# Three parts of a down projection as seven products of quarters, begun three steps late, in a two-layer hybrid trunk on one core

## The chip, the cores and the metric

The kernel runs on one core of one Trainium2 chip. The metric is the device time of one execution in microseconds (us). A profiled execution has, beside its time, a span (first to last instruction), busy times of the engines and the granted clock of the matmul engine. The engines are TensorE (PE; its weight loads are shown as PEld), VectorE (DVE), ScalarE (ACT), GpSimd (POOL) and SyncE (SP). SP and POOL issue the DMAs, and POOL's DMAs can add to what stands in SBUF. Each engine works through its own queue in order.

## The reference, cut to what matters

The trunk has two layers, each a mixer followed by a gated FFN with a short convolution. There are 576 columns (512 of a prompt and 8 sequences of 8), a model width of 1024 and an FFN width of 2816.

```python
for layer in (0, 1):
    x = x + mixer[layer](rmsnorm(x))         # 0: conv module and window attention; 1: Mamba-2
    h = rmsnorm(x)
    g = causal_depthwise_conv3(h @ w_gate)   # 1024 -> 2816
    x = x + (silu(g) * (h @ w_up)) @ w_down  # 2816 -> 1024
```

The change is in how the last product, `@ w_down`, is computed.

## The kernel before, in words

**Layout.** Features lie on partitions, the 576 columns on the free axis. The residual `x` is 8 tiles of 128x576 in float32 (`x[0]` to `x[7]`; in the rows of the order they are `x0_77` to `x7_84`). The FFN width is 22 tiles, numbered f. `HALF` cuts the columns in two halves of 288. A product in float32 is three matmuls on rounded parts (fp32r): high x high, high x low, low x high, where the low half is the original minus the high one. A split is thus one ScalarE copy (the high half) and one VectorE subtraction (the low half).

**Order of the work.** The Python code runs through the instructions in some order, and a tile scheduler with priorities orders each engine's queue. `keep_in_program_order` holds the first matmul of a product in its place.

**Gate and up** (`ffn`, L546). The first tiles (f 0 to 3 of gate, 0 and 1 of up) are done directly at the start. The others go in pairs of f, one job each (`Gate`, `Up`), by the class `Strassen`: quarters of the weights (two f tiles, the two halves of the 1024 rows) times quarters of `h` (halves of rows, halves of columns) in seven products `p1` to `p7` of 12 matmuls (L113, L116, L117), instead of eight. 84 matmuls make a job. The sums of weights are made by DMA: SP loads a quarter into a slot (L68), POOL's accumulating DMA adds the other (L69). `split` (L82, L83) makes the high and low halves, `wl` and `dl` being the low ones. The products accumulate in PSUM banks that are held, `x` and `y`, and in `z`; `keep` (L120) copies intermediate values into SBUF, and the job's `c11`, `c12`, `c22`, `c21` combine them. A pair of jobs (gate of f, f+1 and up of f-2, f-1) yields two more f tiles of silu(gate) x up, the tiles `gsilu`.

**Down.** The 22 f tiles fall into six `PARTS`: f 0 to 1, 2 to 5, 6 to 9, 10 to 13, 14 to 17, 18 to 21. When a part's last tile is there, the loop over the jobs starts its generator `down(p)` (L699): 8 output tiles, each with its own weights (`weights_load` L273, a ring of three buffers `wr`; `single` L293 and L294, two buffers `vh` and `vl`), each in two halves of columns with 4 x 3 matmuls (`mm3` L313, L316, L317), and `add_x` (L497), which adds a PSUM bank to the residual. The generator yields after each half. The loop calls it through `some(1)` four times in a job, so a part takes four jobs, the next part's jobs, while its matmuls stand between the products of gate and up. `up_done` (L581) splits each finished `gsilu` into the pair `yh`, `yl` (L335, L336). The last part goes through `out_proj`, behind the loop.

**SBUF.** `S` hands out slots of 128x576 float32, first in, first out: 48, and 14 more (`EXTRA`) from the first FFN on, 62 in all. Small tiles (`Z`) and the constants of the second mixer (`cst`, 876 columns, loaded through SP at L227, whose second load comes at 172.8 us, before the first FFN begins) are in a pool of their own. The history of the short convolution (`fhist`, `chist`) and the tails that are given back (`fso`, `cso`) have a slot each.

Of the kernel before, what the change touches and what calls it, by code (L numbers as in the profile page):

```python
# [8 lines left out]
F32 = mybir.dt.float32  # L9
F32R = mybir.dt.float32r  # L10
AF = mybir.ActivationFunctionType
# [3 lines left out]
P = 128  # L15
NP = 512
T = 576
HB = 288
DM = 1024
NF = 22  # L20
# [3 lines left out]
LEAD_G, LEAD_U = 4, 2  # L24
PARTS = ((0, 2), (2, 6), (6, 10), (10, 14), (14, 18), (18, 22))


# [13 lines left out]
CV, _n = {}, 0  # L41
# [7 lines left out]
NCV = _n  # L49
# [108 lines left out]
class Builder:  # L158
    NSLOT = 48
    EXTRA = 14  # L160

    def __init__(self, nc, tc, d, stack):
        self.nc, self.tc, self.d = nc, tc, d
        self.const = stack.enter_context(tc.tile_pool(name="const", bufs=1))
        self.xp = stack.enter_context(tc.tile_pool(name="xp", bufs=1))
        self.wp = stack.enter_context(tc.tile_pool(name="wp", bufs=1))
        self.sp = stack.enter_context(tc.tile_pool(name="sp", bufs=1))
        self.pp = stack.enter_context(tc.tile_pool(name="pp", bufs=1, space=bass.MemoryType.PSUM))
        self.dp = stack.enter_context(tc.tile_pool(name="dp", bufs=1, space=bass.MemoryType.DRAM))
        self.rings = {"mm": [0, 1, 2, 3], "aux": [4, 5, 6, 7]}  # L170
        self.idle = list(range(self.NSLOT))
        self.used = {}
        self.held = {}


    def S(self, name, n=T, dt=F32, rows=P):

        i = self.idle.pop(0)
# [11 lines left out]

    def Z(self, name, n, rows=P, bufs=2):
        return self.zp.tile([rows, n], F32, tag=name, bufs=bufs, name=name)

# [23 lines left out]
    def cv(self, name, i=0, n=None, rows=P):  # L217
        o = CV[name] + i
        return self.cst[0:rows, o - self.cst0:o - self.cst0 + n]

    def phase(self, pool, first, last):

        self.zp, self.cst0 = pool, CV[first]
        self.cst = pool.tile([P, (CV[last] if last else NCV) - CV[first]], F32, name="cst")

    def constants(self):
        self.nc.sync.dma_start(self.cst, self.d["cst"][:, self.cst0:self.cst0 + self.cst.shape[-1]])  # L227

# [317 lines left out]
    def ffn(self, l, next_norm):  # L546
        nc, d = self.nc, self.d
        self.rings = {"mm": [0, 1, 2, 3, 4, 5], "aux": [6, 7]}
        hist, so = self.S("fhist", NF * 16), self.S("fso", NF * 16)
        nc.sync.dma_start(hist, d["ffn_hist"][l])  # L550
# [12 lines left out]
        def gate_done(f):  # L563
# [15 lines left out]
            self.free(g, cv)  # L579

        def up_done(f):  # L581
            y_of[f] = self.pair("y")
            self.split(sl_of[f], y_of[f])
            self.free(sl_of.pop(f))

# [113 lines left out]
        def down(p):  # L699
            a, b = PARTS[p]  # L700
            ys = [y_of[f] for f in range(a, b)]
# [10 lines left out]
            def go():  # L712
                nonlocal w
                for m in range(8):
                    now = w
                    if m < 7:
                        w = ready(m + 1)
                    for half in (0, 1):
                        t = self.pm()
                        self.mm3(t[:, :HB], now, range(b - a), ys, HALF[half], pin=True)  # L720
                        self.add_x(m, half, t)
                        if m == 7 and half == 1:
                            self.free([y_of.pop(f) for f in range(a, b)])
                        yield
            return go()

# [13 lines left out]
        for n, job in enumerate(todo + [None]):  # L740
# [42 lines left out]
        nc.sync.dma_start(d["ffn_p"][l], po)  # L783
        self.free(so, hist, self.sr, list(self.hq.values()))
        if next_norm:
            self.norm_begin(*next_norm)
        a, b = PARTS[-1]
        self.out_proj([[d["w_down"][l, m + i][:, a * P:b * P] for i in (0, 1)] for m in range(0, 8, 2)], [y_of[f] for f in range(a, b)],
# [4 lines left out]
    def mix0(self):  # L793
# [181 lines left out]
        self.rings = {"mm": [0, 1, 2, 3], "aux": [4, 5, 6, 7]}  # L975
        self.constants()
        l2 = self.zp.tile([P, P], F32R, tag="l2r", bufs=1, name="l2r")
# [289 lines left out]
    def mix1(self):  # L1267
        nc, d = self.nc, self.d
        hist, so = self.S("chist"), self.S("cso")
        nc.sync.dma_start(hist, d["cc_hist"])  # L1270
# [470 lines left out]
        nc.sync.dma_start(d["cc_p"], po)  # L1741
        self.free(so, hist)
        self.norm_end()
# [7 lines left out]
def build(nc, tc, d):  # L1751
    from contextlib import ExitStack
    with ExitStack() as stack:
        b = Builder(nc, tc, d, stack)
        b.setup()
        with tc.tile_pool(name="segp", bufs=1) as b.segp:
            b.phase(b.segp, "h32", "tri")
# [3 lines left out]
        b.phase(b.ep, "tri", None)  # L1761
        b.ffn(0, ("norm_o", False))
        b.constants()
        b.mix1()
# [159 lines left out]
```

## Time and profile before

| what | value |
|---|---|
| time, median of 3 runs | 1482.84 us (1482.15 to 1484.68) |
| profiled execution: time / span | 1483.3 / 1481.5 us |
| mean granted clock of PE | 0.995 |
| busy: PE, DVE, ACT, POOL | 1459.2, 1119.0, 822.0, 304.1 us |
| matmuls in the trace | 11179 |
| HBM read / written | 190.54 / 15.21 MB |
| matmuls of the down products (`vh`, L313) | 576, from 266.4 to 1452.0 us |

The page gives an engine's busy time, the span in 40 slices, the DMA queues, the chain that ended last and the costliest groups of instructions. In a group, `L313 PE MATMUL mm<-yh,vh` is the line of the kernel, engine, operation, and what it writes from what it reads (buffer numbers left out). Then come the count, busy time, mean duration in ns, and the idle time of the engine just before these instructions, with what ended it. In a timeline, the first two columns are start and duration in us. A row of the table by stage has, for each engine, busy time and number of instructions, then the granted clock of PE (1.00 is full), the DMA share and GB/s.

### The profile page before, as it was taken

Reading aid. Unit: us, or ns where it says so; the run is one execution under the profiler, and the core shown is the slowest. Engines: PE = TensorE matmul, PEld = TensorE weight load, DVE = VectorE, ACT = ScalarE, POOL = GpSimd, SP = SyncE. Lnnn points to the kernel's source line nnn. Section 1 sums busy time; section 2 is a strip of 40 time slices with the busy share of each in tenths; the row PEclk is TensorE's granted clock in tenths of the full one; section 3 lists DMA queues with packets and bytes.
Section 4 is the critical chain, followed back from the end, with each engine's and each line's share of the span. In section 5 each row is a group of like instructions: output and inputs, shape, how many; then the busy total and the mean of one; then the engine's idle time right before and its main releaser. Section 6 shows DMA issues by size and latency. Waiting matters only on the chain.

```text
span 1481.5 us, 29273 instructions
## 1 busy us (share of the span) xinstructions
PE 1459.2 (99%) x11179; PEld 1389.9 (94%) x11179; DVE 1119.0 (76%) x2121; ACT 822.0 (55%) x1659; POOL 304.1 (21%) x517
## 2 busy tenths in 40 slices
PE   8999999999999999999999999999999999999999
PEld 7967799999999999998988998997999999999998
DVE  7968799876666665878897777776989766666673
ACT  6357467655445543487764665665457554444450
POOL 0026211222222220011203102102022222232300
PEclk9999999999999999999999999999999999999999
DMA  7604553787777772136245245245366787877841
GB/s 228 164 29 118 160 133 100 195 212 197 184 200 197 191 191 69 58 121 199 72 154 178 86 124 165 86 146 166 105 172 176 193 217 184 211 195 179 212 113 65
DMA packets 120779, 227.60 MB, mean 154 GB/s; under 512 B 25518, under 2 KB 32558, under 8 KB 120638
## 3 DMA queue, kind: packets, MB, share of 16 engines
q1 hardware_dynamic: 98750, 185.87, 39.7%
q0 software_dynamic: 21888, 39.86, 16.3%
q8 instruction: 88, 1.44, 0.4%
q14 instruction: 53, 0.43, 0.1%
HBM read 190.54 MB, written 15.21 MB: 139 GB/s over the span
## 4 chain that ended last, share of the span: by engine, by line
PE 86%; DVE 6%; ACT 4%; DMA 2%; issue 1%; SPq 0%; ACTq 0%; POOL 0%; DVEq 0%
PE mm L313 15%; PE mm L317 15%; PE mm L316 15%; PE x L113 5%; PE x L116 5%; PE x L117 5%; PE y L116 3%; PE y L117 3%; PE y L113 3%; PE mm L622 2%; PE mm L618 2%; PE mm L621 2%; PE z L116 1%; PE z L113 1%; PE z L117 1%; DMA acb<-acd 1%
## 5 line engine op out<-in xcount | busy, mean ns | idle before, releaser
L313 PE MATMUL mm<-hh,wh 128*128 128x288 f32 x864 | 261.0, 303 | 6.0 <-ACT wh L284 5.4
L316 PE MATMUL mm<-hl,wh 128*128 128x288 f32 x864 | 258.8, 300 | 0.9 <-DVE hl L801 0.8
L317 PE MATMUL mm<-hh,wl 128*128 128x288 f32 x864 | 257.5, 298 | 0.5 <-DVE wl L285 0.5
L497 DVE TENSOR_TENSOR x<-x,mm 128x288 f32<-128x288 f32 x288 | 128.6, 449 | 77.6 <-PE mm L317 76.3
L313 PEld LDWEIGHTS mm<-hh,wh 128*128 128x128 f32 x864 | 163.6, 190 | 14.3 <-ACT wh L284 5.9
L313 PE MATMUL mm<-yh,vh 128*128 128x288 f32 x576 | 170.0, 295 | 0.0
L316 PE MATMUL mm<-yl,vh 128*128 128x288 f32 x576 | 169.9, 295 | 0.0
L317 PE MATMUL mm<-yh,vl 128*128 128x288 f32 x576 | 169.8, 295 | 0.0
L316 PEld LDWEIGHTS mm<-hl,wh 128*128 128x128 f32 x864 | 163.5, 189 | 4.4 <-issue 1.6
L317 PEld LDWEIGHTS mm<-hh,wl 128*128 128x128 f32 x864 | 163.6, 189 | 3.5 <-issue 1.6
L284 ACT ACTIVATE wh<-wr 128x1024 fp32r<-128x1024 f32 (+1 forms) x97 | 101.6, 1048 | 102.6 <-PE mm L316 79.0
L285 DVE TENSOR_TENSOR wl<-wr,wh 128x1024 fp32r<-128x1024 f32 (+1 forms) x97 | 119.5, 1236 | 36.3 <-ACT wh L284 35.5
L82 ACT ACTIVATE wh<-st 128x512 fp32r<-128x512 f32 x152 | 91.3, 626 | 57.8 <-PE z L116 36.0
L69 POOL DMA_DIRECT2D st<-st x76 | 67.5, 889 | 262.8 <-DMA st<-st 65.5
L313 PE MATMUL mm<-yh,wh 128*128 128x288 f32 x384 | 115.9, 302 | 0.7 <-DVE x L497 0.7
L317 PE MATMUL mm<-yh,wl 128*128 128x288 f32 x384 | 115.0, 300 | 0.0
L316 PE MATMUL mm<-yl,wh 128*128 128x288 f32 x384 | 114.9, 300 | 0.0
L83 DVE TENSOR_TENSOR wl<-st,wh 128x512 fp32r<-128x512 f32 x152 | 101.3, 688 | 15.9 <-ACT wh L82 12.3
L316 PEld LDWEIGHTS mm<-yl,vh 128*128 128x128 f32 x576 | 108.4, 188 | 0.0
L317 PEld LDWEIGHTS mm<-yh,vl 128*128 128x128 f32 x576 | 108.3, 188 | 0.0
L313 PEld LDWEIGHTS mm<-yh,vh 128*128 128x128 f32 x576 | 108.3, 188 | 0.0
L573 DVE SCALAR_TENSOR_TENSOR gconv<-gbuf,par,gconv 128x592 f32<-128x592 f32 x88 | 73.0, 832 | 32.2 <-ACT gconv L571 31.6
(409 smaller groups left out, 4306.4 us busy)
## 6 DMA issues: line engine op xcount, KB each, us to landing
st<-in_w_up SPq DMA_DIRECT2D x80, 256.0 KB, 4.3
wr<-in_w_down SPq DMA_DIRECT2D x80, 256.0 KB, 3.5
wr<-in_w_in_o SPq DMA_DIRECT2D x40, 512.0 KB, 3.6
st<-st POOLq DMA_DIRECT2D x76, 256.0 KB, 4.7
st<-in_w_gate SPq DMA_DIRECT2D x72, 256.0 KB, 4.6
wr<-in_w_gate SPq DMA_DIRECT2D x26, 512.0 KB, 4.3
wr<-in_w_up SPq DMA_DIRECT2D x24, 512.0 KB, 4.1
st<-in_w_up POOLq DMA_DIRECT2D x40, 256.0 KB, 4.7
```

The source lines that it names most:

```text
L82: nc.scalar.activation(hi, src, AF.Copy)
L83: nc.vector.tensor_tensor(lo, src, hi.bitcast(F32), op=SUB)
L113: m = nc.tensor.matmul(out, hi[:, ws], xh, start=first and k == 0, stop=False, skip_group_check=skip)
L116: nc.tensor.matmul(out, hi[:, ws], xl, start=False, stop=False, skip_group_check=skip)
L117: nc.tensor.matmul(out, lo[:, ws], xh, start=False, stop=k == 3, skip_group_check=skip)
L284: nc.scalar.activation(hi[:, a:b], raw[:, a:b], AF.Copy)
L285: nc.vector.tensor_tensor(lo[:, a:b], raw[:, a:b], hi[:, a:b].bitcast(F32), op=SUB)
L313: first = nc.tensor.matmul(out, hi[:, ws], xh[:, sl], start=i == 0, stop=False)
L316: nc.tensor.matmul(out, hi[:, ws], xl[:, sl], start=False, stop=False)
L317: nc.tensor.matmul(out, lo[:, ws], xh[:, sl], start=False, stop=i == n - 1)
L497: nc.vector.tensor_tensor(self.x[m][:, sl], self.x[m][:, sl], p[:, :HB], op=ADD)
L573: nc.vector.scalar_tensor_tensor(cv[:, :592], g[:, k:592 + k], w(k), cv[:, :592], op0=MUL, op1=ADD)
```

## The change

Parts 1, 2 and 3 (f 2 to 5, 6 to 9, 10 to 13), in both layers, go through a new generator `down7` in place of `down`.

*Products.* Two output tiles m, m+1 and the part's two halves of f (two tiles each) make four quarters of weights: A11 and A12 are tile m from the first and the second half of f, A21 and A22 tile m+1. The operand's quarters B11, B21 (first and second half of f, first 288 columns), B12, B22 (second 288 columns) are the part's `gsilu`. Seven products of two blocks, 6 matmuls each (`product`, L773, L776, L777 in the changed kernel), do for a pair of output tiles: with A11 on B11 (bank `dx`) and A12 on B21 (bank `mm`); with the first sums of weights on T1 (bank `dy`) and on T2 (`dx`); with the second sums on B22 (`dy`) and on T3 (`dx`); and with A22 on T4 (`dx`). `dx` and `dy` accumulate over several of them, and `add` (L818) adds or subtracts the bank's state behind a product: seven additions of 288 columns for a pair of output tiles, where there were four.

*Operands.* `operand` (L597, L599, L601) writes a high and a low half of 288 columns into one slot (`yq`, or `yT` for the sums T1 to T4, which `combine`, L795, makes in place from the `gsilu` tiles). `up_done` does only the first half of a part's f tiles for such a part; the rest is done by the generator. While a seven-product part runs, the operands of the next part's first half wait until it is over (`waiting`).

*Weights.* `sums` makes two tiles of sums (`sd`) with four additions of 256 columns, and the high and low half of A22 (`dd`, L836). `single` (L306, L307) splits A11 with A12, and each `sd`.

*Three steps late.* The generator yields three times before its first product, while sums and operands are formed.

*SBUF.* `EXTRA` is 19, 67 slots in all, and the added slots of even number hold at most 576 columns, which `S` heeds. `hist` and `so` are one tile in the FFN and in the second mixer. That mixer's small tiles are cut from slots (`small`), its constants stand in two slots (520 and 356 columns) and are loaded when it begins, on SP's queue behind four of the eight last loads of w_down.

```diff
-    EXTRA = 14
+    EXTRA = 19
...
-        hist, so = self.S("fhist", NF * 16), self.S("fso", NF * 16)
+        hist = so = self.S("fhist", NF * 16)
...
+        def operand(name, src, sign=1.0):
+            q = self.S(name, T, F32R)
+            hi, lo = q[:, 0:HB], q[:, HB:T]
+            nc.scalar.activation(hi, src, AF.Copy, scale=sign)
...
+                nc.vector.tensor_tensor(lo, src, hi.bitcast(F32), op=SUB)
...
+        def down7(p):
+            a, b = waiting(p)
+            c = (a + b) // 2
...
+            def sums(m):
+                a11, a12, a21, a22 = [raw[m][:, i * n:i * n + n] for i in range(4)]
+                s12, s43 = s[m, 2], s[m, 3] = self.S("sd", 2 * n), self.S("sd", 2 * n)
+                nc.vector.tensor_tensor(s12[:, 0:n], a21, a22, op=ADD)
+                nc.vector.tensor_tensor(s12[:, n:2 * n], s12[:, 0:n], a11, op=ADD)
+                nc.vector.tensor_tensor(s43[:, n:2 * n], a11, a21, op=ADD)
+                nc.vector.tensor_tensor(s43[:, 0:n], a12, s12[:, n:2 * n], op=ADD)
...
+            def fourth(m):
+                d = last.pop(m)
+                product(x[m][:, :HB], (d[:, 0:n], d[:, n:2 * n]), 0, t["T4"], False)
+                add(m + 1, 0, x[m], SUB)
...
+                sums(0)
+                yield
+                quarters_of("B22")
+                quarters_of("T2")
+                yield
+                split(0, 2)
+                yield
+                for m in range(0, 8, 2):
+                    if m:
+                        fourth(m - 2)
+                    x[m], z = self.ps("dx"), self.pm()
+                    product(x[m][:, :HB], w[m, 1], 0, t["B11"], True)
+                    add(m, 0, x[m], ADD)
+                    product(z[:, :HB], w[m, 1], n, t["B21"], True)
+                    add(m, 0, z, ADD)
+                    split(m, 3)
...
+                    yield
+                    y = self.hold("dy")
+                    product(y[:, :HB], w[m, 2], 0, t["T1"], True)
+                    add(m + 1, 1, y, SUB)
+                    product(x[m][:, :HB], w[m, 2], n, t["T2"], False)
+                    add(m, 1, x[m], ADD)
...
+                    yield
+                    product(y[:, :HB], w[m, 3], 0, t["B22"], False)
+                    add(m, 1, y, ADD)
+                    self.give(y)
+                    product(x[m][:, :HB], w[m, 3], n, t["T3"], False)
+                    add(m + 1, 1, x[m], SUB)
+                    if m < 6:
+                        sums(m + 2)
+                        split(m + 2, 2)
+                    yield
+                fourth(6)
...
-                tiles = down(ready)
+                tiles = (down7 if ready in SEVEN else down)(ready)
...
-        hist, so = self.S("chist"), self.S("cso")
+        self.constants(lambda n: self.S("cst", n), "tri", "selm", None)
+        self.small = []
+        hist = so = self.S("chist")
```

In the built program PE has 10405 matmuls and other entries where it had 10549, DVE 2445 instructions in place of 2121, ACT 1691 in place of 1583, POOL 517 as before, and SP 636 in place of 635.

PE before, the second half of the first output tile of part 1 in layer 0 (`yh`, `yl` are the operand's halves for the four f tiles, `vh`, `vl` the weights'):

```order
L313 MATMUL mm_4153<-yh_3569,vh_4064 128x288
L316 MATMUL mm_4153<-yl_3570,vh_4064 128x288
L317 MATMUL mm_4153<-yh_3569,vl_4065 128x288
L313 MATMUL mm_4153<-yh_3668,vh_4064 128x288
L316 MATMUL mm_4153<-yl_3669,vh_4064 128x288
L317 MATMUL mm_4153<-yh_3668,vl_4065 128x288
L313 MATMUL mm_4153<-yh_3952,vh_4064 128x288
L316 MATMUL mm_4153<-yl_3953,vh_4064 128x288
L317 MATMUL mm_4153<-yh_3952,vl_4065 128x288
L313 MATMUL mm_4153<-yh_4044,vh_4064 128x288
L316 MATMUL mm_4153<-yl_4045,vh_4064 128x288
L317 MATMUL mm_4153<-yh_4044,vl_4065 128x288
```

PE after, the third step of the first pair of output tiles of the same part: the product with B22 (`yq_4149`, `yq_4152`) into `dy` and the one with T3 (`yT_4241`, `yT_4244`) into `dx`:

```order
L773 MATMUL dy_4326<-yq_4149,vh_4237 128x288
L776 MATMUL dy_4326<-yq_4149,vh_4237 128x288
L777 MATMUL dy_4326<-yq_4149,vl_4238 128x288
L773 MATMUL dy_4326<-yq_4152,vh_4237 128x288
L776 MATMUL dy_4326<-yq_4152,vh_4237 128x288
L777 MATMUL dy_4326<-yq_4152,vl_4238 128x288
L773 MATMUL dx_4221<-yT_4241,vh_4237 128x288
L776 MATMUL dx_4221<-yT_4241,vh_4237 128x288
L777 MATMUL dx_4221<-yT_4241,vl_4238 128x288
L773 MATMUL dx_4221<-yT_4244,vh_4237 128x288
L776 MATMUL dx_4221<-yT_4244,vh_4237 128x288
L777 MATMUL dx_4221<-yT_4244,vl_4238 128x288
```

Twelve matmuls on four f tiles that ended in one bank are now two products of six that go on in two banks begun earlier. Behind these rows come the 12 matmuls of `p7` of an up job, and then the product with `dd_4120` (A22 on T4), again into `dx_4221`.

DVE before, from the addition behind these matmuls (the second of that part) to the fourth (`gbuf` and `gconv` belong to a gate job, `st` and `gsilu` also to an up job, `vl` and `wl` are low halves of weights):

```order
L497 TENSOR_TENSOR x0_77<-x0_77,mm_4153 128x288
L573 SCALAR_TENSOR_TENSOR gconv_4146<-gbuf_3999,par_72,gconv_4146 128x592
L641 SCALAR_TENSOR_TENSOR gbuf_4179<-st_3160,x_3912 128x224
L642 SCALAR_TENSOR_TENSOR gbuf_4179<-st_3160,x_3912 128x8x8
L294 TENSOR_TENSOR vl_4188<-wr_4184,vh_4187 128x512
L83 TENSOR_TENSOR wl_4306<-wr_4289,wh_4305 128x1024
L497 TENSOR_TENSOR x1_78<-x1_78,mm_4191 128x288
L659 TENSOR_TENSOR st_3159<-st_3159,z_4205 128x288
L83 TENSOR_TENSOR wl_4310<-st3_4073,wh_4309 128x512
L661 TENSOR_TENSOR gsilu_3761<-gsilu_3761,st_3159 128x288
L83 TENSOR_TENSOR wl_4310<-st2_4072,wh_4309 128x512
L497 TENSOR_TENSOR x1_78<-x1_78,mm_4240 128x288
```

DVE after, from the addition that reads `dy_4326` behind the product with B22 to the split of the next `sd`:

```order
L818 TENSOR_TENSOR x0_77<-x0_77,dy_4326 128x288
L818 TENSOR_TENSOR x1_78<-x1_78,dx_4221 128x288
L307 TENSOR_TENSOR vl_4394<-sd_4381,vh_4393 128x512
L699 SCALAR_TENSOR_TENSOR st_3158<-st_3158,x_4100 128x288
L84 TENSOR_TENSOR dl_4547<-wr_4534,dh_4546 128x512
L703 TENSOR_TENSOR gsilu_3862<-gsilu_3862,st_3158 128x288
L818 TENSOR_TENSOR x1_78<-x1_78,dx_4221 128x288
L818 TENSOR_TENSOR x2_79<-x2_79,dx_4418 128x288
L84 TENSOR_TENSOR wl_4537<-wr_4520,wh_4536 128x1024
L818 TENSOR_TENSOR x2_79<-x2_79,mm_4419 128x288
L307 TENSOR_TENSOR vl_4435<-sd_4382,vh_4434 128x512
```

In the rows before, four or five other instructions stand between two additions to the residual; now additions stand in pairs, and low halves of sums (`vl<-sd`) between them. Row five of the last fence is a split for another job, row seven the addition behind the product with A22.

More of the change, by code (lines that the diff above doesn't have):

```diff
@@ L25 @@
 PARTS = ((0, 2), (2, 6), (6, 10), (10, 14), (14, 18), (18, 22))
+SEVEN = (1, 2, 3)
 PV, _n = {}, 0
@@ L172, in __init__ @@
         self.used = {}
+        self.small = None
         self.held = {}
     def S(self, name, n=T, dt=F32, rows=P):
-        i = self.idle.pop(0)
+        i = next((i for i in self.idle if n <= T or i % 2), self.idle[0])
+        self.idle.remove(i)
         pool = self.sp if i < self.NSLOT else self.ep
@@ L191, in Z @@
     def Z(self, name, n, rows=P, bufs=2):
+        if self.small is not None:
+            fits = [s for s in self.small if s[1] + n <= T]
+            if not fits:
+                self.small.append([self.S("small"), 0])
+            s = (fits or self.small[-1:])[0]
+            s[1] += n
+            return s[0][0:rows, s[1] - n:s[1]]
         return self.zp.tile([rows, n], F32, tag=name, bufs=bufs, name=name)
@@ L218, in cv, with constants @@
         o = CV[name] + i
[L219 to L227, printed above, removed]
+        a, t = next((a, t) for a, b, t in self.cst if a <= o and o + (n or 1) <= b)
+        return t[0:rows, o - a:o - a + n]
+    def constants(self, tile, *names):
+        self.cst = []
+        for a, b in zip(names, names[1:]):
+            a, b = CV[a], CV[b] if b else NCV
+            t = tile(b - a)
+            self.nc.sync.dma_start(t, self.d["cst"][:, a:b])
+            self.cst.append((a, b, t))
     def setup(self):
@@ L724, in go, with product @@
                         yield
+            return go()
+        def product(out, w, col, xs, first):
+            hi, lo = w
+            for k, q in enumerate(xs):
+                ws = slice(col + k * P, col + k * P + P)
+                m = nc.tensor.matmul(out, hi[:, ws], q[:, 0:HB], start=first and k == 0, stop=False, skip_group_check=not first)
+                if k == 0:
+                    self.tc.keep_in_program_order(m)
+                nc.tensor.matmul(out, hi[:, ws], q[:, HB:T], start=False, stop=False, skip_group_check=not first)
+                nc.tensor.matmul(out, lo[:, ws], q[:, 0:HB], start=False, stop=k == len(xs) - 1, skip_group_check=not first)
@@ L783, in ffn @@
         nc.sync.dma_start(d["ffn_p"][l], po)
-        self.free(so, hist, self.sr, list(self.hq.values()))
+        self.free(hist, self.sr, list(self.hq.values()))
         if next_norm:
             self.norm_begin(*next_norm)
-        a, b = PARTS[-1]
+        a, b = waiting(len(PARTS) - 1)
         self.out_proj([[d["w_down"][l, m + i][:, a * P:b * P] for i in (0, 1)] for m in range(0, 8, 2)], [y_of[f] for f in range(a, b)],
@@ L975, in mix0 @@
         self.rings = {"mm": [0, 1, 2, 3], "aux": [4, 5, 6, 7]}
-        self.constants()
+        self.constants(lambda n: self.zp.tile([P, n], F32, name="cst"), "h32", "tri")
         l2 = self.zp.tile([P, P], F32R, tag="l2r", bufs=1, name="l2r")
@@ L1741, in mix1 @@
         nc.sync.dma_start(d["cc_p"], po)
-        self.free(so, hist)
+        self.free(hist, [s[0] for s in self.small], [t for _, _, t in self.cst])
+        self.small = None
         self.norm_end()
@@ L1756, in build @@
         with tc.tile_pool(name="segp", bufs=1) as b.segp:
-            b.phase(b.segp, "h32", "tri")
+            b.zp = b.segp
             b.mix0()
@@ L1760, in build @@
         b.idle += range(b.NSLOT, b.NSLOT + b.EXTRA)
-        b.phase(b.ep, "tri", None)
+        b.zp = b.ep
         b.ffn(0, ("norm_o", False))
-        b.constants()
         b.mix1()
```

81 lines of the change are left out of this document (77 added, 4 removed).

## The prediction

> **What bounds the kernel now.** I read the page first (busy time, then the chain that ended last), then a table by stage, then single instructions. Busy time and chain:
>
> ```profile
> PE 1459.2 (99%) x11179; PEld 1389.9 (94%) x11179; DVE 1119.0 (76%) x2121; ACT 822.0 (55%) x1659; POOL 304.1 (21%) x517
> ...
> PE 86%; DVE 6%; ACT 4%; DMA 2%; issue 1%; SPq 0%; ACTq 0%; POOL 0%; DVEq 0%
> ...
> L313 PE MATMUL mm<-yh,vh 128*128 128x288 f32 x576 | 170.0, 295 | 0.0
> ```
>
> TensorE (PE) ends the span, and the last row, the first of the three matmuls of a down product, shows no idle time before any of its 576. Its mean of 295 ns is not what one matmul costs, though, because successive ones overlap. The timeline of PE gives the start times:
>
> ```profile
> 311.47 0.30 PE L113 MATMUL y<-hqB,wh 128*128 128x288 f32 x1
> 311.60 0.30 PE L116 MATMUL y<-hqB,wh 128*128 128x288 f32 x1
> 311.73 0.30 PE L117 MATMUL y<-hqB,wl 128*128 128x288 f32 x1
> 311.87 0.30 PE L313 MATMUL mm<-yh,vh 128*128 128x288 f32 x1
> ```
>
> They start 0.13 us apart. The table by stage has three stretches of 70 us of the first FFN (down products beside the gate and up jobs), the FFN's opening (220 to 260), a stretch of the first mixer (40 to 60) and the second mixer (600 to 1060). Its columns are PE, weight loads, DVE, ACT, POOL, granted clock, DMA:
>
> ```profile
> 40.00:60.00 20.00, 19.60 (x154) 18.49 (x153) 19.69 (x34) 6.83 (x13) 1.21 (x3) 1.00 0.64 138
> 220.00:260.00 40.00, 39.96 (x305) 39.45 (x305) 38.75 (x84) 28.54 (x65) 6.35 (x10) 1.00 0.32 93
> 340.00:410.00 70.00, 70.00 (x530) 70.00 (x529) 46.91 (x85) 34.79 (x63) 20.85 (x34) 1.00 0.77 194
> 410.00:480.00 70.00, 70.00 (x529) 70.00 (x529) 46.47 (x85) 34.59 (x63) 19.70 (x32) 1.00 0.78 197
> 480.00:550.00 70.00, 70.00 (x529) 70.00 (x528) 46.18 (x85) 34.84 (x62) 18.80 (x30) 1.00 0.78 191
> 600.00:1060.00 460.00, 451.59 (x3479) 414.17 (x3478) 369.00 (x649) 292.58 (x627) 71.47 (x125) 1.00 0.40 129
> ```
>
> In the FFN PE never idles and its clock is full: 70.00 us hold 530 matmuls, 0.132 us each. Whatever takes matmuls out of there shortens the span by 0.132 us apiece, as long as VectorE (DVE), busy 46.5 of 70 us, can feed it. That condition is the whole question.
>
> **The change part by part.** I sum against the profiled execution, 1483.3 us (span 1481.5 and 1.8 around it); the median of the runs is 1482.84, so 0.5 comes off at the end.
>
> *Matmuls.* Before, a part of four f tiles has 8 output tiles x 2 halves x 12 = 192 matmuls, 48 for each pair of output tiles. Seven products of quarters have 7 x 6 = 42. That is 6 fewer for each of 4 pairs, 3 parts and 2 layers: 144. At 0.132 us: **-19.0 us**. The Trainium skill, in "TensorE: Matmul & The Clock Gate", Back-to-back issue gap, gives N / 2.4 + 2.5 ns for an isolated warm matmul, an estimate of 122.5 ns for N = 288; by it this term would be 17.6. The trace's 0.132 is 8% longer and decides.
>
> *VectorE.* Per part the diff adds: 4 third splits of 512 columns, 5 x 4 = 20 operations of 256 on weights, 12 additions of 288 to the residual (28 instead of 16), 14 low halves of operands and 8 sums of operands, of 288 each; it removes 4 splits of 576. That is 54 more. What one costs in a full queue is the distance of starts, from a stretch where DVE is never idle:
>
> ```profile
> 250.04 1.21 DVE L83 TENSOR_TENSOR wl<-wr,wh 128x1024 fp32r<-128x1024 f32 x1
> 251.17 0.68 DVE L83 TENSOR_TENSOR dl<-wr,dh 128x512 fp32r<-128x512 f32 x1
> 251.78 0.41 DVE L294 TENSOR_TENSOR vl<-wr,vh 128x256 fp32r<-128x256 f32 x1
> 252.11 0.44 DVE L408 TENSOR_TENSOR hqT<-hf,hqT 128x288 fp32r<-128x288 f32 x1
> 252.48 0.44 DVE L601 TENSOR_TENSOR gsilu<-mm,gsilu 128x288 f32<-128x288 f32 x1
> 252.86 1.29 DVE L83 TENSOR_TENSOR wl<-st,wh 128x512 fp32r<-128x512 f32 x2
> 254.07 0.75 DVE L336 TENSOR_TENSOR yl<-gsilu,yh 128x576 fp32r<-128x576 f32 x1
> 254.74 0.45 DVE L408 TENSOR_TENSOR hqT<-hf,hqT 128x288 fp32r<-128x288 f32 x1
> ```
>
> So 256 columns take 0.33 us, 288 take 0.37, 512 take 0.61, 576 take 0.67, 1024 take 1.13; the duration beside them is some 0.08 longer, which the next instruction covers. The sum is 20 x 0.33 + 4 x 0.61 + 34 x 0.37 - 4 x 0.67 = 18.9 us per part. A part lasts four jobs: 528 matmuls before (69.7 us), 504 after (66.5). DVE then needs 46.5 + 18.9 = 65.4 of 66.5 us. That is the upper end: many of the 85 instructions of a stretch stand alone and count their 0.08 of cover, at most 85 x 0.08 = 6.8 us, so the lower end is 58.6. I take 62 to 65, 93 to 98%.
>
> The nearest row to that is 220 to 260: DVE at 38.75 of 40 (97%), PE at 39.96 with 305 matmuls, no loss. The row against it is 40 to 60: DVE at 98%, PE 0.40 of 20 us idle, 2%. Over six parts of 66.5 us the loss lies between 0 and 8 us, and not below 0, since PE cannot beat its own pace. I take 3, nearer the row that has the FFN's own operations: **+3 us**.
>
> *The waits that it adds.* The seven products accumulate in two banks (`dx`, `dy`) and DVE reads each partial sum before the next product may go on. The shortest distance is from the seventh product to the fourth, with only the 12 matmuls of one gate or up product between (1.58 us); by the order it occurs twice in a part, 12 times in all. The other distances are 18 matmuls or more. The way there and back is in these rows, with the last matmul of `y` at 311.73 (above):
>
> ```profile
> 312.07 0.46 DVE L659 TENSOR_TENSOR st<-st,y 128x288 f32<-128x288 f32 x1 [0.96 <-PE y L117]
> ...
> 320.86 0.46 DVE L672 SCALAR_TENSOR_TENSOR gsilu<-x,gsilu 128x288 f32<-128x288 f32 x1 [0.37 <-PE x L117]
> ...
> 321.35 0.69 ACT L335 ACTIVATE yh<-gsilu 128x576 fp32r<-128x576 f32 x1 [1.59 <-DVE gsilu L672]
> ```
>
> 0.34 us from the matmul's start to DVE's, 0.46 for the addition, 0.03 to whoever waits for it: 0.83, against 1.58 + 0.13 from the last matmul's start to the next that needs the bank. 0.9 is spare, so an addition (0.37) or a 512 split (0.61) ahead of it in DVE's queue does no harm, and the order has nothing longer there. Cost 0; if a 1024 split (1.13) got in front, 0.2 to 0.4 us each. Behind a waiting addition DVE's queue holds the next weight splits; PE uses those only a product or more later, so they are the cover.
>
> *ScalarE.* It gains 18 operations per part: 4 of 512, 4 of 256, 14 of 288, less 4 of 576. The groups of the three stretches:
>
> ```profile
> L293 ACT ACTIVATE vh<-wr 128x512 fp32r<-128x512 f32 x24 | 15.0, 624 | 7.9 <-PE mm L316 6.5 <-DMA wr<-in_w_down 1.1 <-ACT st L120 0.2
> L120 ACT ACTIVATE st<-x 128x288 f32<-128x288 f32 x24 | 9.5, 394 | 0.9 <-PE x L117 0.9
> L335 ACT ACTIVATE yh<-gsilu 128x576 fp32r<-128x576 f32 x12 | 8.2, 686 | 23.6 <-DVE gsilu L661 14.1 <-DVE gsilu L672 9.5
> ```
>
> With no row of 256 there, I price it as 288: 4 x 0.62 + 18 x 0.39 - 4 x 0.69 = 6.8 us. With 34.8 that is 41.6 of 66.5 us, hidden by PE.
>
> *Transfers.* w_down is read in as many pieces as before, so the DMA share of 0.77 only rises to 0.81. The chains of stored sums are what can be late:
>
> ```profile
> st<-st POOLq DMA_DIRECT2D x76, 256.0 KB, 4.7
> st<-in_w_gate SPq DMA_DIRECT2D x72, 256.0 KB, 4.6
> ...
> L83 DVE TENSOR_TENSOR dl<-wr,dh 128x512 fp32r<-128x512 f32 x12 | 8.3, 690 | 23.5 <-ACT dh L82 16.2 <-DMA st<-st 7.3
> ```
>
> Load plus accumulation is 9.3 us. Counting tiles taken and given back through the code, the fewest idle slots in the loop are four in both kernels: the five new ones go to the new operands. DVE already waits for such chains (7.3 us of 210) without PE noticing; with less slack some will show: between 0 and the 7.3, **+1 us**.
>
> *The start of a part.* In its first three steps the products stand still and PE has only the jobs' 84 matmuls; the quarters are formed behind them. It is inside the sum for DVE above. *History and tail tile in one:* POOL's copies go in the same order, 0. *Mixer:* the constants are now loaded into slots and stand ahead of the last w_down loads on SP's queue, behind reads of finished jobs; who needs them is `pt<-cst` at 617 us, some 50 us after those loads:
>
> ```profile
> 563.66 3.04 SPq L273 DMA_DIRECT2D wr<-in_w_down  x4
> ...
> L1330 PE MATMUL pt<-cst,dtr x8: 190/275/276, 617.3 to 635.9; 128*128 128x32 f32 x8
> ```
>
> 0 while that distance covers it. DVE's order in the mixer shifts in places; PE idles 460 - 451.59 = 8.4 us there, of which a few may come or go: 0, bounds -2 and +3.
>
> Sum: 1483.3 - 19.0 + 3 + 1 = 1468.3, and against the median **1468 us**. All costs at 0 give 1463.8.
>
> **The rivals.** *A. VectorE becomes the bound, and slower (0.08).* The mechanism is that DVE, in order, keeps the wait at `dl` for ScalarE and the chain: 23.5 us of 210, 7.8 per part. If it stays whole on top of 65.4, a part takes 73.2 instead of 69.7: +3.5 x 6 = 21, **1504 us**. It decides from 1.1 us of kept waits per part on, and the kernel is slower from 4.3 on. Against it: such waits exist because DVE is early, and a busier DVE arrives later.
>
> *B. VectorE pays the whole duration (0.08).* With 0.41, 0.69, 0.45 and 0.75 us for the four sizes, the addition is 8.2 + 2.8 + 15.3 - 3.0 = 23.3, a part 69.8 us where it was 69.7: the gain is gone, **1483 us**. Against it is the distance of starts above. The Trainium skill says this in "VectorE: DVE Perf Modes", The TRN2 errata: a fixed latency is exposed between instructions, and many small tiles pay it each time, fp32 `tensor_tensor` costing (N + 151) / 0.96 ns. By that, cutting products into quarters is the wrong way; the trace agrees with its 691 ns for 512 (the `dl` row has 690) as a duration, not as a spacing.
>
> *C. The turnarounds stall (0.14).* Weight splits come in front of the additions at the 12 tight places and as often at the next ones: 24 x 0.3 = 7 us more, **1475 us**. For it: a split of 1024 (1.21 us) comes once in every job. Against it: the order.
>
> *D. The change doesn't do what it says.* The built order has 144 fewer matmuls, so no chance is given to it.
>
> **How the numbers follow.** Forecast 0.70 (1464 to 1473), C 0.14, B 0.08, A 0.08. Faster than 0.2% (3 us, about what a measurement of this kernel can tell from no change): forecast and C, 0.84; same: B, 0.08; slower: A, 0.08. The range runs from the full gain with a little from the mixer, 1463, to C with the mixer's bound, 1478; it leaves A and B out.
>
> **What would show it.** Right: in the FFN PE still full in every 20 us, some 150 matmuls each, DVE at 17.5 to 19.5 of 20 beside the new products; the parts 66.5 us long, the two FFNs 9 us shorter each, the mixers as before. A would show as PE waiting on `vl` or `wl` with DVE waiting on `dh`; B as DVE without idle time and starts 0.45 apart; C as PE waiting at `dx` for DVE. The forecast is wrong if PE loses over 2 us per part, or if the second mixer moves by over 3.

## The result and the profile after

The changed kernel took 1508.51 us (median of 4 runs, 1503.02 to 1512.86), the kernel before 1482.49 in the same comparison: a ratio of 1.0175, 95% interval 1.0153 to 1.0197. It is slower by 1.75%. The profiled execution, the fastest of the four, took 1503.02 us, its span is 1501.2. One execution of `sixty_nine_slots` below, 1731.28 us at a granted clock of 0.753, was in a slower state, and its ratio leaves it out. The page and the table by stage of the changed kernel, for the stretches shown of before:

```profile
PE 1450.3 (97%) x11035; PEld 1376.0 (92%) x11035; DVE 1220.6 (81%) x2445; ACT 856.4 (57%) x1771; POOL 319.0 (21%) x517
```

```profile
340.00:410.00 70.00, 66.41 (x491) 66.20 (x490) 59.41 (x130) 39.13 (x78) 19.88 (x29) 0.98 0.72 172
410.00:480.00 70.00, 67.95 (x500) 67.56 (x499) 62.72 (x138) 39.21 (x80) 19.88 (x32) 0.98 0.77 193
480.00:550.00 70.00, 65.01 (x483) 63.88 (x481) 52.36 (x108) 32.22 (x61) 17.41 (x29) 1.00 0.80 207
```

The 144 matmuls are gone (11035 in place of 11179), but where PE had 530 matmuls in 70 us it now has 483 to 500. It is idle, its clock is below full in two stretches of three, and VectorE, the suspected bound, is less busy (52 to 63 of 70) than the sum said.

The loss lies in the two FFNs. I measure the loop of an FFN from the first matmul of its first job (`x<-hqB`) to the first of its last part (`mm<-yh,wh`). Before, the two loops took 326.8 and 326.2 us, now 342.4 and 332.8; the stretch between them took 541.0 and 541.1. These lengths, here and below, are those of one profiled execution each. Whom PE waits for, in the first loop from 290 us on (two stalls lie ahead, of 1.3 and 1.8 us) and in the second (us in total, times, longest):

```profile
PE dy L773 <- DVE x L818: 7.9, 3, 3.6
PE y L114 <- DVE gbuf L678: 5.5, 1, 5.5
PE dx L773 <- DVE x L818: 2.2, 3, 1.1
```

```profile
PE dx L773 <- DVE x L818: 5.4, 5, 1.7
PE dy L773 <- DVE x L818: 3.4, 2, 2.0
PE z L114 <- DVE x L510: 2.1, 2, 1.5
PE x L114 <- DVE gbuf L684: 0.4, 1, 0.4
```

Most waits are for an addition that reads `dy` or `dx`; before, PE waited for nobody in the loops. One of the waits, followed back through the timelines of SP, POOL, ScalarE, VectorE and PE:

```profile
332.44 1.40 SPq L69 DMA_DIRECT2D st<-in_w_gate  x2
...
335.85 0.86 POOL L70 DMA_DIRECT2D st<-st  x1 [3.11 <-DMA st<-in_w_gate]
...
342.41 0.63 ACT L83 ACTIVATE wh<-st 128x512 fp32r<-128x512 f32 x1 [3.72 <-DMA st<-st]
...
343.07 0.69 DVE L84 TENSOR_TENSOR wl<-st,wh 128x512 fp32r<-128x512 f32 x1 [2.98 <-ACT wh L83]
343.68 0.45 DVE L818 TENSOR_TENSOR x<-x,dy 128x288 f32<-128x288 f32 x1
...
344.28 0.58 PE L773 MATMUL dy<-yq,vh 128*128 128x288 f32 x1 [3.59 <-DVE x L818]
344.65 0.44 PE L776 MATMUL dy<-yq,vh 128*128 128x288 f32 x1
344.89 0.44 PE L777 MATMUL dy<-yq,vl 128*128 128x288 f32 x1
```

PE waits for an addition whose bank had long been ready; it stood behind `wl<-st`, a split for another job, which waited for ScalarE, which waited for a stored sum. That accumulation was issued at 335.85 and landed some 6.5 us later. Then PE goes on at half speed (0.24 us from start to start). Followed back in this way, each of the 20 stalls of over 0.25 us in the two loops ends at a transfer: a stored sum (`st`) or the low quarter of a job's weights (`dh<-wr`). In eight of them, 8.7 us in all, the transfer had landed 6 to 13 us before PE went on, and the full queues of VectorE and ScalarE carried the delay: there their load has a part. The stalls add up to 33.8 us, and 17.1 us of the loops run at half clock, which costs some 8 more (0.24 us from start to start in place of 0.13).

VectorE waits less at `dl` than before (7.7 us in place of 23.5 in 210), as I had argued. What is new is a wait for stored sums, first on ScalarE. The groups of 340 to 550, before and after:

```profile
L82 ACT ACTIVATE wh<-st 128x512 fp32r<-128x512 f32 x48 | 28.9, 625 | 18.5 <-PE z L116 15.6 <-PE x L116 2.6
```

```profile
L83 ACT ACTIVATE wh<-st 128x512 fp32r<-128x512 f32 x44 | 26.4, 623 | 25.9 <-DMA st<-st 8.0 <-PE x L117 7.5 <-DMA st<-in_w_up 7.3
...
L84 DVE TENSOR_TENSOR dl<-wr,dh 128x512 fp32r<-128x512 f32 x12 | 8.2, 686 | 7.7 <-ACT dh L83 7.7
```

Before, ScalarE waited for PE there, and the sums lay ready; now 15.3 of 25.9 us are waits for transfers. (For the low quarters, `dh<-wr`, ScalarE waited 45.6 us in the two loops before too, without a stall of PE; now 60.7.)

### The profile page after: what moved, and what is told of

Its sections match the earlier page's. It is cut to its first block, busy times and chain, and to the rows that moved or that the text cites. A ratio compares the mean times of both kernels' runs of the same rounds, so it can differ in the third digit from the quotient of the medians.

```text
span 1501.2 us, 29480 instructions
## 1 busy us (share of the span) xinstructions
PE 1450.3 (97%) x11035; PEld 1376.0 (92%) x11035; DVE 1220.6 (81%) x2445; ACT 856.4 (57%) x1771; POOL 319.0 (21%) x517
## 3 DMA queue, kind: packets, MB, share of 16 engines
q1 hardware_dynamic: 98894, 185.87, 38.9%
q0 software_dynamic: 21888, 39.86, 16.1%
## 5 line engine op out<-in xcount | busy, mean ns | idle before, releaser
L510 DVE TENSOR_TENSOR x<-x,mm 128x288 f32<-128x288 f32 x192 | 85.1, 449 | 43.4 <-PE mm L330 42.7
L114 PE MATMUL x<-hqT,wh 128*128 128x288 f32 x304 | 90.6, 298 | 0.0
L117 PE MATMUL x<-hqT,wh 128*128 128x288 f32 x304 | 90.4, 297 | 0.0
L118 PE MATMUL x<-hqT,wl 128*128 128x288 f32 x304 | 90.1, 296 | 0.0
L326 PEld LDWEIGHTS mm<-yh,wh 128*128 128x128 f32 x384 | 72.3, 188 | 3.5 <-issue 1.8
L330 PEld LDWEIGHTS mm<-yh,wl 128*128 128x128 f32 x384 | 72.3, 188 | 1.0 <-issue 0.4
L329 PEld LDWEIGHTS mm<-yl,wh 128*128 128x128 f32 x384 | 72.3, 188 | 0.5 <-issue 0.2
```

The costliest lines, as they stand in the source:

```text
L114: m = nc.tensor.matmul(out, hi[:, ws], xh, start=first and k == 0, stop=False, skip_group_check=skip)
L117: nc.tensor.matmul(out, hi[:, ws], xl, start=False, stop=False, skip_group_check=skip)
L118: nc.tensor.matmul(out, lo[:, ws], xh, start=False, stop=k == 3, skip_group_check=skip)
L326: first = nc.tensor.matmul(out, hi[:, ws], xh[:, sl], start=i == 0, stop=False)
L329: nc.tensor.matmul(out, hi[:, ws], xl[:, sl], start=False, stop=False)
L330: nc.tensor.matmul(out, lo[:, ws], xh[:, sl], start=False, stop=i == n - 1)
```

## The experiments

Eighteen kernels. Theory L: transfers land late, and the in-order queues of ScalarE and VectorE carry that to the additions. Theory D, the rival: VectorE's load by itself.

### The other edits, one part alone, the transfers, the load

`slots_only` has `SEVEN = ()`, `only_part_2` has `SEVEN = (2,)`.

> All edits of the change but the seven products: no part goes through them. Both theories put the loss into the three parts, so both expect the time of before, 1480 to 1486 us, with 0.5 % as the limit; 1490 or more would say that the slots, the constants or the shared history cost something by themselves.

> Part 2 alone (f 6 to 9) in seven products. Full gain of two parts of 48 matmuls less 24 each: 2 x 24 x 0.132 = 6.3 us. Theory L (late stored sums: the loads wait for slots that come back late, ScalarE and VectorE wait for the sums, the additions stand behind): fewer tiles are alive with neighbours of the old form, so part of the stalls goes, 1478 to 1486. Theory D (VectorE's load by itself): a third of the loss of the change, about +8, 1488 to 1493.

```diff
plain_sums
-            self.nc.gpsimd.dma_start(s, more, accum_op=ADD)
before_48_adds
                         self.add_x(m, half, t)
+                        if p in (1, 2, 3):
+                            for op in (SUB, ADD) * (2 - half):
+                                x = self.x[m][:, HALF[half]]
+                                nc.vector.tensor_tensor(x, x, t[:, :HB], op=op)
```

> The change, with POOL's accumulating DMAs left out: the stored sums of weights are plain quarters, so gate and up are not the reference's. Slots, TensorE, VectorE and ScalarE have the same work. Theory L: the chain load, accumulation, accumulation is gone, so the long stalls (3.6 and 5.5 us in the first FFN) go with the half-clock windows behind them: 1470 to 1485. Theory D: no change against the change, 1500 to 1512. Stalls at the bank of the fourth product stay by both.

> The kernel before with 48 more additions of 288 columns in each of the three parts (each PSUM bank taken off the residual and added again, once or twice): 48 x 0.37 = 17.8 us of VectorE per part, near the 18.9 of the change, and no slot more. Theory L: slots and loads as before, PE loses little, 1483 to 1488. Theory D: VectorE at 92 % makes the waits, 1495 to 1510.

| kernel | us | ratio to before (95%) | loops 1 and 2, us |
|---|---|---|---|
| slots_only | 1483.69 | 1.0012 (1.0000 to 1.0024) | 330.4, 327.5 |
| only_part_2 | 1503.87 | 1.0148 (1.0133 to 1.0163) | 339.5, 337.9 |
| plain_sums | 1463.17 | 0.9874 (0.9859 to 0.9888) | 316.8, 316.8 |
| before_48_adds | 1487.36 | 1.0036 (1.0021 to 1.0052) | 330.1, 326.2 |

Without the accumulations the whole gain is there, below the range expected: the loops are 10.0 and 9.4 us shorter than before. The change's are 25.6 + 16.0 = 41.6 us longer than these, which is what its stalls and its half clock come to. The table by stage of `plain_sums`:

```profile
340.00:410.00 70.00, 70.00 (x531) 70.00 (x530) 65.76 (x142) 41.82 (x82) 5.73 (x16) 1.00 0.42 137
410.00:480.00 70.00, 69.77 (x527) 69.57 (x526) 65.68 (x142) 42.95 (x84) 4.17 (x16) 1.00 0.42 136
480.00:550.00 70.00, 70.00 (x530) 70.00 (x530) 56.40 (x111) 36.62 (x66) 4.22 (x14) 1.00 0.40 128
```

VectorE is at 94% in the first two stretches and PE loses 0.23 of 210 us. D falls here, and once more with `before_48_adds`, where a load of 85 to 92% in the same stretches costs 5 us. What fell is the DMA share, from 0.72 to 0.80 to 0.42, and POOL's busy time, which held the issuing of the accumulations (its time for one is the same before and after, 0.92 us in the mean). The surprise is `only_part_2`: by neither theory did one part cost nearly as much as three. Its waits in the first loop:

```profile
PE y L114 <- DVE gbuf L678: 5.0, 1, 5.0
PE z L114 <- DVE x L510: 4.6, 3, 2.1
PE dx L773 <- DVE x L818: 1.3, 2, 0.8
```

Most stalls stand outside the new products (`y`, `z`), and three of them (at 283, 300 and 349 us) lie in the parts ahead of part 2. Followed back, those three end at low quarters that landed 5.4 to 8.3 us after their issue. The first of them stands in `slots_only` too (2.7 us at 284), whose loops are 3.6 and 1.3 us longer than before though its time is not: the other edits move the low quarters as well.

### Length of the chain, bytes, slots, the low quarter

`before_12_slots` has `EXTRA = 12` in the kernel before.

```diff
one_link
-        ... (s2, up[:, 0:512], s1), (s4, up[:, 512:1024], s2), ...
+        ... (s2, up[:, 0:512], low[:, 512:1024]), (s4, up[:, 512:1024], low[:, 0:512]), ...
part_sums
-            self.nc.gpsimd.dma_start(s, more, accum_op=ADD)
+            self.nc.gpsimd.dma_start(s[:, 0:128], more[:, 0:128], accum_op=ADD)
low_split_later
-            elif new:
+            elif n == 0:
                 new.sums()
...
                 new.p2()
+                if n > 1:
+                    new.sums()
low_in_slot
-        self.low = b.weights_load(low[:, 512:1024], 512)
+        self.low = b.S("low", 512)
+        self.nc.sync.dma_start(self.low, low[:, 512:1024])
...
+        b.free(self.low)
two_more_slots
-    EXTRA = 19
+    EXTRA = 21
...
-        i = next((i for i in self.idle if n <= T or i % 2), self.idle[0])
+        fit = [i for i in self.idle if (n <= 512 or i < self.NSLOT + 9) and (n <= T or i % 2)]
+        i = next((i for i in fit if n <= 512 and i >= self.NSLOT + 9), fit[0])
```

> The change, with each of the four stored sums made of a load and one accumulation from HBM: none waits for another sum (two of the four sums lack a term or have another, so gate and up are not the reference's). As many DMAs of the same size, slots as in the change. If the length of the chain (load, accumulation, accumulation on the first's result) is what makes the sums late: 1463 to 1475 us, as with plain sums. If it is the bytes in the queues, that the accumulations take from the urgent loads: 1495 to 1510.

> The change, with the accumulating DMAs cut to 128 of their 512 columns: as many of them, as many links and the same waits, a quarter of their bytes (the rest of the stored sums lacks a term, so gate and up are not the reference's). If the load on the DMA engines makes the loads late: 1463 to 1478 us. If it is the number of links, or POOL's queue, whose copies stand between: 1495 to 1512.

> The kernel before with 12 more slots in place of 14 from the first FFN on, 60 in all, and nothing else. If late slots are what makes loads late: slower than before, 1490 to 1505. If slots are not what is short, and the transfers only collide: within 0.3 % of before, 1479 to 1487.

> The change, with the split of each job's low quarter of weights (dh and dl, needed by the job's seventh product only) moved behind the job's second product. VectorE waited for that load ahead of additions in the change and with part 2 alone. If these waits are a large part of the loss: 1485 to 1500. If the stored sums' own waits (wl) make it: 1500 to 1512.

> The change, with each job's low quarter of weights loaded into a slot in place of a buffer of the ring wr. The ring is freer, the slots are one shorter per job. If slots are what is short: slower than the change, 1510 to 1525. If the ring holds SP's queue up: faster, 1485 to 1500.

> The change with 69 slots in place of 67: 12 of the added ones hold 512 columns only, and tiles of up to 512 columns take those first. If slots are short: 1485 to 1500 us. If the load on the DMA engines is what counts: 1500 to 1512, as the change.

| kernel | us | ratio to before (95%) |
|---|---|---|
| one_link | 1515.93 | 1.0238 (1.0213 to 1.0262) |
| part_sums | 1473.97 | 0.9947 (0.9929 to 0.9965) |
| before_12_slots | 1491.23 | 1.0071 (1.0056 to 1.0086) |
| low_split_later | 1509.89 | 1.0191 (1.0164 to 1.0217) |
| low_in_slot | 1518.32 | 1.0264 (1.0240 to 1.0288) |
| two_more_slots | 1542.72 | 1.0396 (1.0361 to 1.0431) |

With the same bytes, a shorter chain brings nothing. With the same chain and a quarter of the bytes, 34.5 of the 45.3 us between the change and `plain_sums` come back. So it is the bytes, not the links: a smaller accumulation lands sooner (`st<-st` after 2.9 us in place of 4.4, medians), and the low quarters, which keep their size, cost ScalarE 17.2 us of waits in the loops in place of 60.7, so the load on the DMA engines counts. Slots count too: two fewer cost the kernel before 10.6 us, about half of it in the stretch between the loops (546.3 us), and one more taken per job cost the change 10. `two_more_slots` misses by a wide margin, and not against slots as such: its narrow slots go first, so each comes round again sooner, and its loads wait: the first load for a job's stored sums is issued 11.8 us (median) ahead of the job's first matmul, in the change 15.6. Splitting the low quarter later did nothing; the waits then end at other transfers.

### POOL in place of the DMAs

```diff
pool_adds, and in the kernel before pool_adds_before
+        self.low = b.weights_load(low[:, 512:1024], 512)
...
-            self.nc.sync.dma_start(s, first)
-            self.nc.gpsimd.dma_start(s, more, accum_op=ADD)
+        self.nc.sync.dma_start(s3, low[:, 0:512])
+        u1, u2 = self.up[:, 0:512], self.up[:, 512:1024]
+        for s, x, y in ((s1, self.low[:, 0:512], s3), (s2, u1, s1), (s4, u2, s2), (s3, u1, s3)):
+            self.nc.gpsimd.tensor_tensor(s, x, y, op=ADD)
```

> The change, with the sums of gate's and up's weights made by four additions of 512 columns on POOL per job (1.25 us each by the nearest row, 5 us of a job's 17) from quarters that are loaded once, in place of eight DMAs, four of them accumulating; the result is the reference's. If the transfers are the cause: nearly the whole gain of the seven products, 1463 to 1472. If slots are: the slots are as many, 1490 to 1510.

> The kernel before with the same edit (POOL's additions for the accumulating DMAs). TensorE loses nothing to transfers in its FFN, so by either theory the time stays within 0.5 %, 1476 to 1488 us.

1557.54 us (1.0513, 1.0483 to 1.0544) and 1500.90 (1.0130, 1.0101 to 1.0159): both expectations missed. The transfers did fall (a DMA share near 0.25), but POOL's additions took 1.58 us each and slowed VectorE, which is the bound in `pool_adds` (266.8 of 280 us from 300 to 580). These two say nothing for or against late transfers; the last section has the rows.

### Turnarounds, load, and slots alone

```diff
own_banks: each product begins a bank of its own, for example
-                    product(x[m][:, :HB], w[m, 2], n, t["T2"], False)
-                    add(m, 1, x[m], ADD)
+                    z = self.ps("dx")
+                    product(z[:, :HB], w[m, 2], n, t["T2"], True)
+                    add(m, 1, z, ADD)
light_vector: no low halves of operands and of A22, the second matmul reads the high half
-                nc.tensor.matmul(out, hi[:, ws], q[:, HB:T], start=False, ...
+                nc.tensor.matmul(out, hi[:, ws], q[:, 0:HB], start=False, ...
fourth_later: fourth(m - 2) behind the pair's first two products, quarters_of("T4") behind the product with T3
fourth_later_low_first: also
+        self.low = b.weights_load(low[:, 512:1024], 512)
         for s, first, more in ((s1, low[:, 512:1024], low[:, 0:512]), (s2, up[:, 0:512], s1), ...
light_packed: light_vector, and
+            tile, col = (half.pop(), HB) if half else (self.S(name, T, F32R), 0)
sixty_nine_slots: the 69 slots of two_more_slots (wide is NSLOT + 9), and
+        if n <= 512 and sum(i < wide for i in fit) <= 6:
+            fit = [i for i in fit if i >= wide] or fit
+        i = fit[0]
```

> The change, with a bank of its own for each of the seven products: none goes on in a bank that an addition reads, so partial sums are missing and the result is not the reference's. TensorE, VectorE, ScalarE and the transfers have the same work. In the change 21.6 of 33.8 us of TensorE's idle time in the two FFNs stood at dx and dy. If the turnarounds make the loss: 1478 to 1490 us. If VectorE cannot catch up, the waits move to other banks: 1497 to 1512.

> The change, with the low halves of the operands' quarters and of A22 left out (the high halves stand in for them, so the result is not the reference's in the last digits): 18 VectorE instructions or 6.5 us per part less, turnarounds and transfers as in the change. If VectorE's load keeps it from catching up: 1475 to 1490. If the turnarounds do it: 1495 to 1512.

> The change, with the fourth product moved behind the next pair's first two, 24 matmuls instead of 12 behind the addition that it waits for, and T4 formed one step later, so that it does not stand ahead of the third product's addition. Turnarounds: the stalls at the fourth product (9.2 us in the profiled run) and those behind T4 (about 6) go, with some half-clock windows: 1485 to 1497. VectorE's load: they move elsewhere, 1500 to 1512.

> The same as fourth_later, and the job's low quarter of weights is loaded ahead of the stored sums instead of behind them. If its late landing makes a good part of the waits: 5 to 10 us below fourth_later; if the stored sums then land later by as much: the same or slower.

> light_vector, with two of the operands' quarters in one slot (their low halves are left out there): 7 slots of a part stay free, 12 idle ones at the least in place of 5 when a stored sum takes its slot; the instructions of all engines and the transfers are those of light_vector. If slots that come back late make the loads late: 1462 to 1480 us. If not: 1495 to 1508, as light_vector.

> The change with 69 slots in place of 67, 12 of them of 512 columns, taken first in, first out, and a narrow one only where 6 or fewer wide ones are idle: 7 idle ones at the least in place of 5. The result is the reference's. If slots are what is short: 1490 to 1503; two of the seven that are short can't give all. If not: 1503 to 1515.

(In `light_vector` and `light_packed` the second matmul counts the high halves twice, so more than the last digits differ.)

| kernel | us | ratio to before (95%) | loops 1 and 2, us |
|---|---|---|---|
| own_banks | 1506.54 | 1.0186 (1.0137 to 1.0235) | 349.1, 341.2 |
| light_vector | 1502.86 | 1.0144 (1.0125 to 1.0164) | 343.6, 329.9 |
| fourth_later | 1514.55 | 1.0219 (1.0193 to 1.0245) | 350.8, 336.0 |
| fourth_later_low_first | 1505.10 | 1.0156 (1.0138 to 1.0173) | 343.0, 339.7 |
| light_packed | 1488.22 | 1.0045 (1.0023 to 1.0066) | 331.2, 330.8 |
| sixty_nine_slots | 1507.20 | 1.0168 (1.0148 to 1.0189) | 336.6, 323.0 |

Without a turnaround the change is as slow as with it: the stalls only stand at other banks (its profiled execution was the slowest of four, 1520.00 us). With 6.5 us per part less on VectorE it gains 5.6 us of the 45. Seven slots more, with the same instructions, gain another 14.6: a real part, but the expected range is missed, and 25 us to `plain_sums` are left. ScalarE's groups (340 to 550) in `light_vector` and in `light_packed` say why:

```profile
L83 ACT ACTIVATE wh<-st 128x512 fp32r<-128x512 f32 x44 | 26.4, 624 | 25.9 <-DMA st<-st 13.8 <-PE x L117 7.5 <-PE z L117 4.6
L83 ACT ACTIVATE dh<-wr 128x512 fp32r<-128x512 f32 x12 | 7.6, 632 | 21.4 <-DMA wr<-in_w_up 17.4 <-DVE vl L307 2.3 <-DMA wr<-in_w_gate 1.7
```

```profile
L83 ACT ACTIVATE wh<-st 128x512 fp32r<-128x512 f32 x46 | 27.5, 624 | 16.3 <-PE z L117 8.9 <-PE x L117 7.4
L83 ACT ACTIVATE dh<-wr 128x512 fp32r<-128x512 f32 x12 | 7.6, 632 | 28.3 <-DMA wr<-in_w_up 15.7 <-DMA wr<-in_w_gate 6.9 <-DVE vl L307 3.7
```

With slots to spare the sums come in time (no wait for a DMA in the first row). The low quarters, which have a ring of buffers and no slots, come later instead, from 19.1 to 22.6 us of waits. `sixty_nine_slots` has the second loop 3.2 us under the kernel before and the first 9.8 over it, but the stretch between the loops took 554.1 us there against 541.0 of before: with other slots the mixer runs otherwise too. No kernel with the reference's result beat the kernel before.

**What late means.** The timelines of SP and PE say when the loads are issued. In the seventh to the eighteenth job of each FFN, the first load for the stored sums goes out 20.7 us (median) ahead of the job's first matmul in the kernel before, 15.6 in the change and 29.1 in `light_packed`. From issue to landing the transfers, taken together, need about as long as before. The medians of the change (before 4.3, 4.7 and 4.6):

```profile
st<-in_w_up SPq DMA_DIRECT2D x80, 256.0 KB, 5.1
...
st<-st POOLq DMA_DIRECT2D x76, 256.0 KB, 4.4
st<-in_w_gate SPq DMA_DIRECT2D x72, 256.0 KB, 3.1
```

So the sums are late because their loads start some 5 us later, and seven more slots bring the start forward again. `plain_sums` starts them as late (16.3 us ahead), but there a sum is one transfer in place of a chain.

**What stays open.** Bytes and slots are shown to make the sums late, by taking bytes away and by adding slots. For the low quarters it isn't settled why one part makes them as late as three (in the loops of `only_part_2` ScalarE waits 89.5 us for them). That the transfers bunch is no answer: of 64 stretches of 5 us in the first loop, the DMA share is 0.95 or more in 7 to 13 before, by where the first one begins, in 12 to 16 after and in 14 to 19 in `only_part_2`, but also in 15 to 20 in `slots_only`, whose time is that of before. That `fourth_later` is slower than the change isn't explained either.

## Why the prediction was wrong

- **Matmuls, -19.0: right.** Where nothing is late, the loops are 10.0 + 9.4 = 19.4 us shorter (`plain_sums`). The trace's 0.132 us per matmul was the right price. By the formula of the Trainium skill ("TensorE: Matmul & The Clock Gate", Back-to-back issue gap) the gain would be an estimated 17.6; this case's loops are nearer the 19.0.
- **VectorE, 62 to 65 of 66.5 us and +3: the load right, the loss too high.** 65.7 of 70 us in `plain_sums` is 62.4 of 66.5; PE lost 0.23 us in 210.
- **Waits at `dx` and `dy`, 0: right as a cause, not as a place.** 21.6 of the 33.8 us of stalls stand there, but `own_banks` shows that they would stand elsewhere. The 0.9 us to spare hold only while nothing in VectorE's queue waits for a transfer; that I priced the queue by durations alone is part of the next point.
- **Transfers, +1: this is the step that failed.** Its measured size is the difference of the spans of the change and of `plain_sums`, 1501.2 - 1460.1 = 41 us, of which VectorE's own load has a small part (5.6 us come back in `light_vector`). It rested on two readings. "The fewest idle slots in the loop are four in both kernels" counted slots in the order of the code, not when they come free: the operands' quarters hold theirs from a part's start to its end, the loads for the sums go out 15.6 us ahead of their job in place of 20.7, and `light_packed` regains 14.6 us by seven more. And "without PE noticing" took a tolerance of before (23.5 us of waits at `dl`, none of which stopped PE) for one of the change. The DMA share of 0.77 stood in the table by stage; I read it as room for 0.81, not as a queue in which a 256 KB accumulation lands 3.2 to 8.8 us after its issue, as before's do.
- **Mixer, 0: right.** `slots_only` is at 1.0012, and in the change the stretch between the loops is as long as before.
- **The rivals.** A's number (1504) is near the result by luck, its mechanism isn't: the wait at `dl` shrank, as the text against it says, and a wait for stored sums took its place. C named the banks, but not what keeps them. B is out by `plain_sums`, where PE is full beside 62.4 us of VectorE per 66.5; B has 69.8. "Slower" had 0.08, because transfers were no rival at all.

## What to carry to other kernels

Before work is moved to an engine with room, look whether it takes buffers, and how full the DMA engines are where those buffers feed loads: in this kernel, at a DMA share of 0.75 to 0.8 and with buffers that turn round just in time, a few more held buffers made loads late, and an in-order engine hands each late load on to all that stands behind it. To find the cause, take away the bytes, the links, the buffers and the load one at a time; where a stall stands says little about it.

## What the runs showed of the hardware

**Short stalls cost clock.** The table by stage for windows of 3.4 us that hold two stalls of the change, and for those behind them:

```profile
412.30:415.70 3.40, 1.35 (x11) 1.14 (x10) 2.43 (x8) 3.22 (x8) 1.14 (x3) 1.00 1.01 321
415.70:419.10 3.40, 3.40 (x16) 3.40 (x16) 3.40 (x10) 0.68 (x2) 0.85 (x1) 0.50 1.07 272
...
483.90:487.30 3.40, 1.50 (x11) 1.53 (x12) 2.81 (x8) 2.87 (x8) 1.66 (x2) 1.00 0.97 321
487.30:490.70 3.40, 3.02 (x23) 2.81 (x22) 3.40 (x10) 1.70 (x2) 0.07 (x1) 1.00 1.08 248
```

A stall of some 2 us within a window put the whole next window at half clock: 14 starts 0.24 us apart in place of 26, some 1.5 us more. A like stall 70 us later did not: 0.4 us of it fell into the window before, and 1.50 us of its own window were busy in place of 1.35. The windows stand in a grid: the half-clock stretches of the two loops begin at 344.00, 415.68, 552.21 and 1292.90 us, all whole multiples of 3.413 us apart. So the cost depends on where a stall falls, and the runs of the change, which spread over 10 us, differ in it (clock 0.988 at 1512.86 us, 0.994 at 1503.02). The Trainium skill, in "TensorE: Matmul & The Clock Gate", Part 1, has free-running windows of about 3.4 us with half clock after an idle one; the trace agrees on length and clock, but here the window was not wholly idle.

**POOL's additions slow VectorE where both its inputs lie in SBUF.** Groups from 340 to 550, before and in `pool_adds_before`:

```profile
L497 DVE TENSOR_TENSOR x<-x,mm 128x288 f32<-128x288 f32 x48 | 21.6, 450 | 16.4 <-PE mm L317 16.4
...
L294 DVE TENSOR_TENSOR vl<-wr,vh 128x512 fp32r<-128x512 f32 x24 | 16.5, 687 | 0.5
...
L661 DVE TENSOR_TENSOR gsilu<-gsilu,st 128x288 f32<-128x288 f32 x18 | 8.2, 453 | 0.3
```

```profile
L294 DVE TENSOR_TENSOR vl<-wr,vh 128x512 fp32r<-128x512 f32 x25 | 27.5, 1101 | 0.2
...
L497 DVE TENSOR_TENSOR x<-x,mm 128x288 f32<-128x288 f32 x48 | 21.5, 448 | 6.8 <-PE mm L317 6.7
...
L661 DVE TENSOR_TENSOR gsilu<-gsilu,st 128x288 f32<-128x288 f32 x18 | 14.6, 810 | 0.3
```

The two with SBUF inputs take 1.6 and 1.8 times as long; the one that reads PSUM takes what it took. The Trainium skill says in "SBUF — State Buffer", SBUF: two separate sides, that a GpSimd operation that reads SBUF and a VectorE operation with two SBUF inputs lock each other out for a whole instruction; these rows agree.

**An accumulating DMA is dear.** On the page of before, POOL's queue moves 39.86 MB in 16.3% of the DMA engines' span, SP's 185.87 MB in 39.7%: 1.9 times the share per byte.
